# Output projection of a hybrid backbone step: its weight pieces split two ahead through a fourth buffer pair, and the down-projection's fourth pair used only from the third step on

## The chip, the cores and the metric

The kernel runs on one core of one Trainium2 chip. The metric is device microseconds of one execution. The kernel before took 3248.36 us, the median of three runs (3247.75, 3248.36 and 3250.61 us). The profile below is of one more execution, which took 3247.33 us; its span, from the first to the last recorded instruction, is 3245.6 us.

## The reference, cut to what matters

One layer of a backbone works on 640 tokens (512 latent tokens and 128 context tokens) of width 2048. The mixer makes `o_a` (RWKV heads, 1024 columns) and `o_b` (gated MLP, 1024 columns). Then come the output projection, a norm and a gated feed-forward of inner width 5632, all in float32:

```
x = x + g1 * (jnp.concatenate([o_a, o_b], axis=-1) @ lp['w_out'])
h = _rmsnorm(x, lp['norm2_g']) * (1.0 + sc2) + sh2
ff = (jax.nn.silu(h @ lp['w_ffn_gate']) * (h @ lp['w_ffn_up'])) @ lp['w_ffn_down']
return x + g2 * ff, s_fin
```

A last RMSNorm follows. The change touches how the weights of `w_out` (its rows for `o_a`) and of `w_ffn_down` are prepared. What is computed stays the same.

## The kernel before, in words

**Number format.** Every float32 operand of a wide matmul is split into a rounded part `hi` and a rest `lo`. ScalarE copies the raw tile into `hi` (`S.copy`, a CAST in the profile), and VectorE subtracts `hi` from the raw tile to give `lo`. Each product is then three matmuls: `hi` of the weights with both parts of the other operand, and `lo` of the weights with its `hi`. In the profile the three have three lines, one for each.

**Pieces.** A piece of weights is a block of 128 columns and up to 512 rows, so a raw tile of 128 x 512 elements. It is loaded by a DMA from SyncE's queue, split, and used by 12 matmuls (4 blocks of 128 rows, three matmuls each, 320 tokens wide), or by 9 where the piece has only 3 blocks. Raw tiles, `hi` and `lo` have three buffers each in a pool called `st`.

**The output projection.** The rows of `w_out` for `o_b` are multiplied earlier, beside the recurrent scan. The stage called the second half here multiplies the other 1024 rows. It loops over two halves `hf` of 320 tokens, over 16 blocks `m` of output columns, and over two pieces `q` of each block, so it handles 64 pieces. Its core is at lines 1661 to 1683:

```
for hf in range(2):
    s = slice(HALF * hf, HALF * hf + HALF)
    for m in range(KB):
        pool = pbig if m % 2 == 0 else pb2
        ps = pool.tile([P, HALF], F32, tag="big", name="big")
        for q in range(2):
            hi, lo = split(w_out[0, 4 * q * P:(4 * q + 4) * P, m * P:(m + 1) * P], 4)
            for k in range(4):
                kb = 4 * q + k
                TE.matmul(ps, hi[:, k, :], o_hi[kb][:, s], start=(kb == 0), stop=False)
                ...
        ...
        add_out(m, [ps, ps], hf)
        ...
        if hf and m % 2:
            first_half(m // 2)
```

`split` (line 391) allocates, loads, casts (398) and subtracts (399). The three matmuls are lines 1670 to 1672. `add_out` (1292) adds the result to the residual `x1T`. After each block the square of the new residual goes into a sum over all columns (ones matmul, line 1654), and when a token half is complete its reciprocal root `rs` is made (1657 to 1659: VectorE, ScalarE, VectorE). In the second token half `first_half(j)` norms the first one: GpSimd multiplies by `rs` (1605), VectorE scales and shifts (1606), and `operand` splits the result (`xo`: ScalarE 1595, VectorE 1596).

The operand blocks `o_hi[kb]`, `o_lo[kb]` (`oh`, `ol` in the profile) come from the scan. The last two, kb = 6 and 7, come out of its last chain: GpSimd norms `Y` (1486), TensorE transposes it into `pO` (1494), VectorE adds it to `bv` (1498), a gate matmul follows (1512, 1513), `bv` is stored to `d_o` (1516) and loaded back as `ol` (1265, split at 1266 and 1267). The first pieces of the stage lie beside this chain.

**The feed-forward.** Both its products are made by a seven-product scheme (four quarter matrices, 7 products, in the order 1, 2, 3, 7, 5, 6, 4). `seven` (matmuls 1826 to 1828) keeps two split pieces ahead of the one in use by calling `parts` (cast 1635, subtraction 1636); GpSimd makes the differences of weights (`t3`, and `raw`, `rawd` in place, line 1730).

`parts` picks the pool: `pool, kw = (gus[-1], dict(bufs=1)) if gus and next(turn4) == 3 else (st, {})`. So while the list `gus` is not empty, every fourth piece gets a fourth pair of buffers, from the last pool in `gus`.

**From gate/up to down.** When the last gate/up step ends, its helper pool `gu` is closed and the memory is used again: by the pool `dh` with the fourth pair for the down-projection (line 2022, put into `gus` at once) and by `dn` with the accumulators `acc`. `gu` held, among others, the tiles `sp` that the last step splits (1946, 1947) and stores with a DMA to `d_os` (1949). The down-projection then runs 48 steps of seven products; in steps 0 and 1 a product is one piece of 9 matmuls. Each product is copied into `acc` (ScalarE 2044, VectorE 2046 the first time), its operands `xd` are loaded (1865, 1871) and split (1878, 1879), and there are eight banks for products.

**What sets the order.** Within this part the code is written in program order and a scheduler of the framework places the instructions on each engine, using a buffer or a bank as soon as it is free in its own plan. Each engine then executes its list in order, and waits are semaphores.

Of the kernel before, what the change touches and what calls it, by code (L numbers as in the profile page):

```python
# [10 lines left out]
F32 = mybir.dt.float32  # L11
F32R = mybir.dt.float32r
# [7 lines left out]
P = 128  # L20
D = 2048
KB = D // P
# [296 lines left out]
def flow_step(ctx: ExitStack, tc, x_prompt, x_sample, state_rwkv, c, c_ctx, w_mod, b_mod,  # L319
# [3 lines left out]
    nc = tc.nc  # L323
    V, S, G, TE = nc.vector, nc.scalar, nc.gpsimd, nc.tensor
# [22 lines left out]
    for h in range(2):  # L347
        s = slice(CH * h, CH * h + CH)
# [40 lines left out]
    st = ctx.enter_context(tc.tile_pool(name="st", bufs=3, side="right"))  # L389

    def split(src, nk):

        n = 512 // nk
        raw = st.tile([P, nk, n], F32, tag="raw", name="raw", bufs=3)
        hi = st.tile([P, nk, n], F32R, tag="hi", name="hi")
        lo = st.tile([P, nk, n], F32R, tag="lo", name="lo")
        nc.sync.dma_start(raw, src.rearrange("(k p) n -> p k n", p=P))
        S.copy(hi, raw)
        V.tensor_sub(lo, raw, hi.bitcast(F32))
        return hi, lo  # L400
# [884 lines left out]
    def add_out(m, halves, hf=None):  # L1285

        for (lo, hi, v) in ((0, HALF, 0), (HALF, LAT, 0), (LAT, T, 1)):
            if hf is not None and lo // HALF != hf:
                continue
            dst = x1T[m][:, lo:hi]  # L1290
            o = HALF * (lo // HALF)
            V.scalar_tensor_tensor(out=dst, in0=halves[lo // HALF][:, lo - o:hi - o], scalar=modc[2][:, m, v:v + 1],
                                   in1=dst, op0=ALU.mult, op1=ALU.add)

    with ExitStack() as ph:
# [17 lines left out]
        for k in (1, 3):  # L1313
            s = slice(32 * k, 32 * k + 32)
# [300 lines left out]
    PW, READY, gus = [], [], []  # L1615
# [23 lines left out]
    with ExitStack() as ph:  # L1639
        np_ = ph.enter_context(tc.tile_pool(name="np", bufs=2))  # L1640
        pss = ph.enter_context(tc.tile_pool(name="pss", bufs=1, space=PSUM))
        pb2 = ph.enter_context(tc.tile_pool(name="pb2", bufs=2, space=PSUM))
        ones = np_.tile([P, P], F32, name="ones", bufs=1)
        V.memset(ones, 1.0)
        V.tensor_scalar_add(modc[4], modc[4], 1.0)
        V.tensor_tensor(out=modc[4], in0=modc[4],
                        in1=prm[:, C_N2:C_N2 + KB].unsqueeze(2).to_broadcast([P, KB, 2]), op=ALU.mult)
        ss = [pss.tile([P, HALF], F32, name=f"ss{hf}") for hf in range(2)]
        sqs = []

        def stats():

            hf, m, sq = sqs.pop()
            TE.matmul(ss[hf], ones, sq, start=(m == 0), stop=(m == KB - 1))
            if m == KB - 1:
                s = slice(HALF * hf, HALF * hf + HALF)
                V.tensor_scalar(rs[:, s], ss[hf], 1.0 / D, RMS_EPS, op0=ALU.mult, op1=ALU.add)
                S.activation(rs[:, s], rs[:, s], AF.Sqrt)
                V.reciprocal(rs[:, s], rs[:, s])

        for hf in range(2):
            s = slice(HALF * hf, HALF * hf + HALF)
            for m in range(KB):
                pool = pbig if m % 2 == 0 else pb2
                ps = pool.tile([P, HALF], F32, tag="big", name="big")
                for q in range(2):
                    hi, lo = split(w_out[0, 4 * q * P:(4 * q + 4) * P, m * P:(m + 1) * P], 4)
                    for k in range(4):
                        kb = 4 * q + k
                        TE.matmul(ps, hi[:, k, :], o_hi[kb][:, s], start=(kb == 0), stop=False)  # L1670
                        TE.matmul(ps, hi[:, k, :], o_lo[kb][:, s], start=False, stop=False)
                        TE.matmul(ps, lo[:, k, :], o_hi[kb][:, s], start=False, stop=(kb == 7))
                if hf and m == KB - 1:
                    for _ in range(3):
                        next(first)
                if sqs:
                    stats()
                add_out(m, [ps, ps], hf)
                nc.sync.dma_start(d_x1[m][:, s], x1T[m][:, s])
                sq = np_.tile([P, HALF], F32, tag="sq2", name="sq2")  # L1680
                S.activation(sq, x1T[m][:, s], AF.Square)
                sqs.append((hf, m, sq))
                if hf and m % 2:
                    first_half(m // 2)
        for _ in range(2):
            READY.append(parts(PW.pop(0)))
        stats()
# [104 lines left out]
    def fresh(i):  # L1792

        return pP.tile([P, 512], F32, tag="P", name=f"P{i}")[:, 0:HALF], False
# [224 lines left out]

    gus.append(ctx.enter_context(tc.tile_pool(name="dh", bufs=1)))
    dn = ctx.enter_context(tc.tile_pool(name="dn", bufs=1))
    acc = dn.tile([P, 8, 7 * HALF], F32, name="acc")
    sse = dn.tile([P, NT, 8], F32, name="sse")
# [26 lines left out]
    def load_x1(n):  # L2052
        if n >= 0:
            xqs[n] = [xap.tile([P, T], F32, tag=f"x1_{(1, 9)[m]}", name="x1d") for m in range(2)]
            for m in range(2):
                nc.sync.dma_start(xqs[n][m], d_x1[2 * n + m])
# [71 lines left out]

    held = {}
    for s, (c, n) in enumerate(steps):  # L2130
        b11, b21, b22, b12 = ([WD.pop((s, b))] for b in ("11", "21", "22", "12"))
        dloads = itertools.chain(dloads, load_down(s + 2))
        final, turn, after = c == NC - 1, s % 8 == 7 and c < NC - 1, s % 8 == 0 and c > 0
        if final or turn and c == NC - 2:
            bank = lambda i, n=n: filled(n, i)
        elif after:
            bank = lambda i: (held[i], True)
        elif turn:
            def bank(i):
                held[i], _ = fresh(i)  # L2140
                return held[i], False
        else:
            bank = fresh
        if c >= NC - 2 and (final or turn):
            lag[0] = LAST_LAG
        then = [(s + 1, b) for b in ("11", "21")] if s + 1 < len(steps) else ()
        for o in seven(b11, b12, b21, b22, lambda i, k: XD[i, k], None if turn else Last(n) if final else Sum(n),
                       CHK[c], bank, not turn, then):
            if turn:
                if o == 1:  # L2150
                    ops = load_ops(c + 1)
                    next(ops)
                if o in AT:
                    next(ops)
            elif s % 8 == 0 and o in BT:
                next(ops)
            if o > 2:
                next(dloads, None)
            if final and after and o == 2:
                load_x1(n)  # L2160
            while later and o >= later[0][0]:
                later.pop(0)[1]()
            if s == len(steps) - 1 and o == 5:
                while hooks:
                    hooks.pop(0)()
# [52 lines left out]
```

## Time and profile before

| | |
|---|---|
| median of three runs | 3248.36 us |
| profiled execution, own time | 3247.33 us |
| profiled execution, span | 3245.6 us |
| TensorE's mean granted clock | 0.978 |
| end of the scan, start of the stage on `w_out` | 1361.4 us in the span |
| last matmul of the sums in that stage | 1525.9 us |
| first matmul of the down-projection | 2629.3 us |
| last one of it | 3218.9 us |

Times are counted from the start of the span. In a timeline a row gives the start, the duration, the engine, the line and what is done; a bracket behind it gives how long the engine sat idle before it and what ended that wait (for a wait on several things, the last one by the profile). In a table of windows each row is a stretch of the span with the busy time of each engine and the number of its instructions, then TensorE's granted clock as a share, the DMA engines' share and GB/s. PE is TensorE, DVE VectorE, ACT ScalarE, POOL GpSimd, SP SyncE.

### The profile page before, as it was taken

The numbers are of one execution on the slowest core, as the hardware profiler recorded it, in microseconds if no ns is written. First come the engines' busy times: TensorE is split into PE (matmuls) and PEld (weight loads), VectorE is DVE, ScalarE is ACT, GpSimd is POOL, SyncE is SP. The second block draws the span as 40 slices with busy tenths as digits, with TensorE's granted clock in tenths as the row PEclk, the third lists the DMA queues.
The fourth block names the chain that finished last, engine by engine and source line by source line (L and its number), as shares of the span: only waits on it lengthen the run. The fifth ranks groups of instructions, "written<-read, shape, count | busy, mean of one in ns | idle before, by whom it ended". The sixth has DMA issues, their size and how long they took to land. (4 is left out here: it accounts for less than half of the span.)

```text
span 3245.6 us, 73506 instructions
## 1 busy us (share of the span) xinstructions
PE 3108.7 (96%) x28828; PEld 2883.5 (89%) x28828; DVE 2322.3 (72%) x4073; ACT 1444.0 (44%) x3161; POOL 1251.2 (39%) x1082
## 2 busy tenths in 40 slices
PE   6899999999998999999999999999999989999996
PEld 3698888888886877798999999999999989999996
DVE  4456767767756576647977787878878777877787
ACT  3244554555543333335644444444444444444365
POOL 0001222222320032302266566656656644555543
PEclk8899999999998999999999999999999999999998
DMA  8768787887986677455434434433343354553453
GB/s 321 254 182 237 208 227 205 235 233 194 234 226 202 206 219 227 148 150 171 126 107 127 127 108 123 122 117 117 119 124 119 108 175 148 160 165 118 137 169 120
DMA packets 741923, 553.01 MB, mean 170 GB/s; under 512 B 141688, under 2 KB 674184, under 8 KB 732744
## 3 DMA queue, kind: packets, MB, share of 16 engines
q1 hardware_dynamic: 729256, 534.62, 55.5%
q0 software_dynamic: 9984, 13.13, 1.7%
q8 instruction: 227, 3.72, 0.5%
q14 instruction: 120, 0.98, 0.1%
q10 hardware_dynamic: 2336, 0.57, 0.1%
HBM read 438.77 MB, written 111.69 MB: 170 GB/s over the span
## 5 line engine op out<-in xcount | busy, mean ns | idle before, releaser
L1828 PE MATMUL P<-xo,lo 128*128 128x320 f32 x2352 | 727.4, 309 | 3.2 <-DVE lo L1636 3.2
L1827 PE MATMUL P<-xo,hi 128*128 128x320 f32 x2352 | 727.9, 309 | 0.0
L1826 PE MATMUL P<-xo,hi 128*128 128x320 f32 x2352 | 727.7, 309 | 0.0
L1636 DVE TENSOR_TENSOR lo<-raw,hi 128x512 fp32r<-128x512 f32 x532 | 512.9, 971 | 162.6 <-ACT hi L1635 160.5
L1635 ACT CAST hi<-raw 128x512 fp32r<-128x512 f32 x532 | 330.2, 622 | 505.1 <-PE P L1827 430.9
L1828 PEld LDWEIGHTS P<-xo,lo 128*128 128x128 f32 x2352 | 441.9, 188 | 3.9 <-DVE lo L1636 3.7
L1826 PEld LDWEIGHTS P<-xo,hi 128*128 128x128 f32 x2352 | 442.2, 188 | 0.0
L1827 PEld LDWEIGHTS P<-xo,hi 128*128 128x128 f32 x2352 | 442.1, 188 | 0.0
L1730 POOL TENSOR_TENSOR raw<-raw 128x512 f32<-128x512 f32 x252 | 413.5, 1644 | 13.6 <-DVE lo L1636 0.6
L106 PE MATMUL big<-h_hi,hi 128*128 128x320 f32 x1280 | 417.8, 326 | 0.9 <-ACT praw L1209 0.9
L1826 PE MATMUL P<-xd,hi 128*128 128x320 f32 x1232 | 382.6, 311 | 17.3 <-DMA rawd<-in_w_ffn_down_dram 12.1
L106 PE MATMUL big<-h_lo,hi 128*128 128x320 f32 x1280 | 394.1, 308 | 0.0
L106 PE MATMUL big<-h_hi,lo 128*128 128x320 f32 x1280 | 394.0, 308 | 0.0
L1828 PE MATMUL P<-xd,lo 128*128 128x320 f32 x1232 | 382.5, 310 | 3.3 <-DVE lo L1636 3.0
L1827 PE MATMUL P<-xd,hi 128*128 128x320 f32 x1232 | 381.6, 310 | 0.0
L1730 POOL TENSOR_TENSOR t<-raw 128x512 f32<-128x512 f32 x84 | 130.7, 1556 | 452.2 <-DMA raw<-in_w_ffn_up_dram 403.6
L1635 ACT CAST hi<-rawd 128x512 fp32r<-128x512 f32 (+1 forms) x288 | 166.2, 586 | 233.5 <-PE P L1827 165.5
L106 PEld LDWEIGHTS big<-h_hi,hi 128*128 128x128 f32 x1280 | 240.7, 188 | 32.7 <-issue 25.9
L1826 PEld LDWEIGHTS P<-xd,hi 128*128 128x128 f32 x1232 | 232.1, 188 | 20.0 <-ACT hi L1635 14.6
L1636 DVE TENSOR_TENSOR lo<-rawd,hi 128x512 fp32r<-128x512 f32 (+1 forms) x288 | 214.1, 749 | 43.6 <-ACT hi L1635 37.4
L106 PEld LDWEIGHTS big<-h_lo,hi 128*128 128x128 f32 x1280 | 240.7, 188 | 1.2
L106 PEld LDWEIGHTS big<-h_hi,lo 128*128 128x128 f32 x1280 | 240.1, 188 | 0.0
(370 smaller groups left out, 6284.3 us busy)
## 6 DMA issues: line engine op xcount, KB each, us to landing
wt<-in_w_mod_dram SPq DMA_DIRECT2D x96, 1024.0 KB
raw<-in_w_ffn_gate_dram SPq DMA_DIRECT2D x182, 256.0 KB
raw<-in_w_ffn_up_dram SPq DMA_DIRECT2D x182, 256.0 KB
rec<-d_S SPq DMA_DIRECT2D x80, 576.0 KB
raw<-in_w_in_dram SPq DMA_DIRECT2D x172, 256.0 KB
rawd<-in_w_ffn_down_dram SPq DMA_DIRECT2D x128, 256.0 KB
raw<-in_w_out_dram SPq DMA_DIRECT2D x96, 256.0 KB
xd<-d_os SPq DMA_DIRECT2D x66, 320.0 KB
```

The lines of the kernel that those rows point to most:

```text
L106: self.eng, self.run = eng, lambda: fn(*args, **kw)
L1635: S.copy(hi[:, 0:nk], raw[:, 0:nk])
L1636: V.tensor_sub(lo[:, 0:nk], raw[:, 0:nk], hi[:, 0:nk].bitcast(F32))
L1730: G.tensor_tensor(out=o[:, 0:nk], in0=p[:, 0:nk], in1=q[:, 0:nk], op=ALU.subtract)
L1826: TE.matmul(ps, hi[:, k, :], xk[:, 0, :], start=f, stop=False)
L1827: TE.matmul(ps, hi[:, k, :], xk[:, 1, :], start=False, stop=False)
L1828: TE.matmul(ps, lo[:, k, :], xk[:, 0, :], start=False, stop=l)
```

## The change

The stage on `w_out` no longer calls `split` at the place of use. A generator makes the pieces, in the same order, and two are always made ahead. Every fourth piece gets its `hi` and `lo` from the stage's own pool `np_` (memory that the scan used before), the others from `st` as before. The raw tiles keep three buffers. In the down-projection `dh` is put into `gus` only at step 2, so the first two steps split into the three pairs of `st` alone.

```
+        def fetched_w():
+            for n in range(4 * KB):
+                raw = st.tile([P, 4, P], F32, tag="raw", name="raw", bufs=3)
+                m, q = divmod(n % (2 * KB), 2)
+                nc.sync.dma_start(raw, w_out[0, 4 * q * P:(4 * q + 4) * P, m * P:(m + 1) * P].rearrange("(k p) n -> p k n", p=P))
+                pool, kw = (np_, dict(bufs=1)) if n % 4 == 3 else (st, {})
+                hi = pool.tile([P, 4, P], F32R, tag="hi", name="hi", **kw)
+                lo = pool.tile([P, 4, P], F32R, tag="lo", name="lo", **kw)
+                S.copy(hi, raw)
+                V.tensor_sub(lo, raw, hi.bitcast(F32))
+                yield hi, lo
+
+        pieces_w = fetched_w()
+        soon = [next(pieces_w) for _ in range(2)]
...
-                    hi, lo = split(w_out[0, 4 * q * P:(4 * q + 4) * P, m * P:(m + 1) * P], 4)
+                    hi, lo = soon.pop(0)
+                    soon.extend(itertools.islice(pieces_w, 1))
...
-    gus.append(ctx.enter_context(tc.tile_pool(name="dh", bufs=1)))
+    dh = ctx.enter_context(tc.tile_pool(name="dh", bufs=1))
...
     for s, (c, n) in enumerate(steps):
+        if s == 2:
+            gus.append(dh)
```

Each engine keeps its number of instructions. Line numbers behind the change grow by 15, and by 17 in the loop of the down-projection. Three places move.

First, TensorE at the end of the scan. `Y` is what GpSimd has normed, `big_19077` is the first output block before, `big_19089` and `big_19172` are the first and the third one now. Before:

```order
L1671 MATMUL big_19077<-ol_18963,hi_19097 128x320
L1672 MATMUL big_19077<-oh_18962,lo_19098 128x320
L1494 MATMUL pO_18983<-I2_68,Y_18079 64x64
L1494 MATMUL pO_18983<-J2_13863,Y_18079 64x64
L1494 MATMUL pO_18983<-I2_68,Y_18079 64x64
```

Now:

```order
L1686 MATMUL big_19089<-ol_18963,hi_19085 128x320
L1687 MATMUL big_19089<-oh_18962,lo_19086 128x320
L1685 MATMUL big_19172<-oh_18937,hi_19133 128x320
L1686 MATMUL big_19172<-ol_18938,hi_19133 128x320
L1494 MATMUL pO_18983<-I2_68,Y_18079 64x64
L1687 MATMUL big_19172<-oh_18937,lo_19134 128x320
L1685 MATMUL big_19172<-oh_18942,hi_19133 128x320
L1686 MATMUL big_19172<-ol_18943,hi_19133 128x320
```

A whole piece (12 matmuls) of the third block moved in front of and among the first transposes of `Y`; a second one (6 of its matmuls) stands between the first 20 and the second 20 transposes, and 3 more matmuls behind them. In all 21 matmuls moved ahead of the gate matmuls of the last chain.

Second, VectorE in the second token half, around the reciprocal root of the first. `lo_19868` is the second piece of block 2 before; now that piece is `lo_19828`, and `lo_19863` is the first piece of block 3. Before:

```order
L399 TENSOR_TENSOR lo_19850<-raw_19848,hi_19849 128x512
L1659 RECIPROCAL rs2_19061<-rs2_19061 128x320
L1292 SCALAR_TENSOR_TENSOR x1T_13831<-big_19794,modc2_83,x1T_13831 128x192
L1292 SCALAR_TENSOR_TENSOR x1T_13831<-big_19794,modc2_83,x1T_13831 128x128
L1606 TENSOR_SCALAR x1T_13832<-x1T_13832,modc4_85,modc3_84 128x320
L1606 TENSOR_SCALAR x1T_13824<-x1T_13824,modc4_85,modc3_84 128x320
L399 TENSOR_TENSOR lo_19868<-raw_19866,hi_19867 128x512
```

Now:

```order
L1670 TENSOR_TENSOR lo_19828<-raw_19825,hi_19827 128x512
L1659 RECIPROCAL rs2_19061<-rs2_19061 128x320
L1292 SCALAR_TENSOR_TENSOR x1T_13831<-big_19806,modc2_83,x1T_13831 128x192
L1292 SCALAR_TENSOR_TENSOR x1T_13831<-big_19806,modc2_83,x1T_13831 128x128
L1606 TENSOR_SCALAR x1T_13832<-x1T_13832,modc4_85,modc3_84 128x320
L1606 TENSOR_SCALAR x1T_13824<-x1T_13824,modc4_85,modc3_84 128x320
L1670 TENSOR_TENSOR lo_19863<-raw_19860,hi_19862 128x512
```

The other work stands where it stood; each subtraction is one piece further on.

Third, ScalarE where the down-projection begins. `hi_33376` belongs to the second product of step 0, `hi_33381`, `hi_33410` and `hi_33430` to the next three, `hi_33446` to the sixth; `sp` are the last tiles of the gate/up stage. Before:

```order
L1635 CAST hi_33381<-rawd_33319 128x384
L1635 CAST hi_33410<-t3_33369 128x384
L1984 ACTIVATE c_33279<-c_33279 128x640
L1635 CAST hi_33430<-rawd_33321 128x384
L1946 CAST sp_33344<-act_33325 128x320
L1946 CAST sp_33349<-act_33089 128x320
L1878 CAST xd_33400<-opd_33240 128x320
L1878 CAST xd_33403<-opd_33240 128x320
L1878 CAST xd_33406<-opd_33242 128x320
L1946 CAST sp_33354<-act_33325 128x320
L1635 CAST hi_33376<-rawd_33283 128x384
L1635 CAST hi_33446<-rawd_33319 128x384
```

Now:

```order
L1635 CAST hi_33376<-rawd_33283 128x384
L1635 CAST hi_33381<-rawd_33319 128x384
L1999 ACTIVATE c_33279<-c_33279 128x640
L1635 CAST hi_33410<-t3_33369 128x384
L1961 CAST sp_33344<-act_33325 128x320
L1635 CAST hi_33430<-rawd_33321 128x384
L1961 CAST sp_33349<-act_33089 128x320
L1893 CAST xd_33400<-opd_33240 128x320
L1893 CAST xd_33403<-opd_33240 128x320
L1893 CAST xd_33406<-opd_33242 128x320
L1635 CAST hi_33446<-rawd_33319 128x384
L1961 CAST sp_33354<-act_33325 128x320
```

The second product's cast moved from behind the last `sp` cast to the front. Behind these rows six products of the step and three of the next are cast before the first copy into `acc`; and one cast of step 2 (the fourth piece of that step, into `dh`) stands in the middle of step 1, ahead of the cast for step 1's fifth product.

## The prediction

> **What bounds the kernel now.** I read the page's busy table first, then windows over the places where the change moves work, then the timeline around each. The busy table:
>
> ```profile
> PE 3108.7 (96%) x28828; PEld 2883.5 (89%) x28828; DVE 2322.3 (72%) x4073; ACT 1444.0 (44%) x3161; POOL 1251.2 (39%) x1082
> ```
>
> TensorE (PE) is busy 96% of the span. The change takes no matmul away, so it can only win time in which PE stands idle or runs at a lower clock. The windows show where that is (start:end, length, busy us with the count for PE, PEld, DVE, ACT, POOL, then granted clock, DMA share, GB/s):
>
> ```profile
> 1376.00:1397.00 21.00, 15.01 (x133) 13.34 (x134) 5.21 (x9) 2.59 (x4) 4.13 (x5) 0.72 0.19 66
> 1450.00:1460.00 10.00, 10.00 (x67) 9.68 (x66) 4.93 (x9) 5.69 (x9) 0.00 (x0) 1.00 0.58 174
> 1460.00:1470.00 10.00, 7.34 (x36) 6.36 (x35) 9.50 (x10) 3.15 (x6) 8.41 (x9) 0.81 0.16 49
> 1470.00:1480.00 10.00, 9.03 (x50) 8.47 (x48) 10.00 (x16) 4.31 (x9) 8.60 (x8) 0.85 0.45 137
> 1478.00:1526.00 48.00, 47.27 (x300) 44.87 (x300) 32.78 (x72) 23.95 (x47) 0.60 (x1) 1.00 0.56 168
> 2630.00:2640.00 10.00, 0.83 (x6) 0.56 (x4) 7.77 (x14) 5.60 (x13) 4.43 (x4) 0.68 0.78 266
> 2640.00:2650.00 10.00, 7.08 (x35) 6.98 (x36) 3.09 (x6) 2.70 (x6) 3.35 (x3) 0.64 0.92 292
> 2650.00:2670.00 20.00, 20.00 (x138) 20.00 (x138) 15.28 (x25) 9.66 (x21) 9.50 (x8) 1.00 0.33 94
> ```
>
> In the stage on `w_out` PE is full around 1455 (one matmul each 10.00/67 = 0.149 us) and loses 0.73 us in the 48 us from 1478 on. There, splitting earlier has almost nothing to win. Its losses are at the end of the scan (row 1) and in the 20 us from 1460. The down-projection runs at one matmul each 20.00/138 = 0.145 us once started, but nearly all of 2630 to 2640 is lost, and after it the clock is low. Gate/up and down both keep PE full afterwards, so what PE wins at any of these three places is carried to the end.
>
> **The end of the scan.** The timeline of all engines there:
>
> ```profile
> 1375.95 0.47 PE L1494 MATMUL pO<-I,Y 64*64 64x64 f32 x2 [4.63 <-POOL Y L1486]
> 1379.75 0.37 PE L1494 MATMUL pO<-J,Y 64*64 64x64 f32 x1 [3.33 <-POOL Y L1486]
> 1395.06 0.72 ACT L1266 CAST oh<-ol 128x640 fp32r<-128x640 f32 x1
> 1395.21 0.41 PE L1670 MATMUL big<-oh,hi 128*128 128x320 f32 x1 [0.56 <-ACT hi L398]
> 1395.82 0.83 DVE L1267 TENSOR_TENSOR ol<-ol,oh 128x640 fp32r<-128x640 f32 x1
> 1398.24 0.31 PE L1672 MATMUL big<-oh,lo 128*128 128x320 f32 x1
> ```
>
> PE waits 4.63 and 3.33 us for GpSimd's `Y`. Before, 6 pieces (72 matmuls, three blocks without their last operands) are through by 1398.24. After, a seventh piece goes into the waits for `Y`: 12 more matmuls, which are then not owed later, 12 × 0.149 = 1.8 us. Against that, 9 of the 21 moved matmuls stand between the transposes and the gate matmuls, so on the chain that makes the last `oh` and `ol`. At the low clock there (0.26 each, worked out in the next part) they take 9 × 0.26 = 2.3 us. About half of it falls into waits of the chain, so I take 1.1. Net: −0.7 us. Bounds: −2.4 if the chain isn't delayed at all and the 0.56 us wait at 1395.21 goes as well; +2.1 if all 2.3 us count and the fourth pair's first cast makes the last `oh` later by a cast and a subtraction (0.72 + 0.83): 2.3 + 1.55 − 1.8.
>
> **The second token half.** The timeline where the first half's norm begins:
>
> ```profile
> 1459.36 2.15 DVE L1659 RECIPROCAL rs<-rs 128x320 f32<-128x320 f32 x1 [1.33 <-ACT rs L1658]
> 1461.59 17.01 POOL L1605 TENSOR_TENSOR x1T<-x1T,rs 128x320 f32<-128x320 f32 x16 [81.22 <-DVE rs L1659]
> 1464.32 1.34 DVE L399 TENSOR_TENSOR lo<-raw,hi 128x512 fp32r<-128x512 f32 x1
> 1465.71 0.42 PE L1672 MATMUL big<-oh,lo 128*128 128x320 f32 x1 [1.91 <-DVE lo L399]
> 1467.73 2.62 DVE L399 TENSOR_TENSOR lo<-raw,hi 128x512 fp32r<-128x512 f32 x2
> 1469.14 0.63 PE L1672 MATMUL big<-oh,lo 128*128 128x320 f32 x1 [0.75 <-DVE lo L399]
> 1477.92 0.41 PE L1672 MATMUL big<-oh,lo 128*128 128x320 f32 x1 [0.97 <-DVE lo L399]
> ```
>
> GpSimd works 17 us at a stretch on `x1T`, and in that time a subtraction takes 1.34 us on VectorE. VectorE is full from 1470 to 1480, and PE waits for `lo` three times: 1.91 + 0.75 + 0.97 = 3.63 us, which is all that PE is idle in the two windows (20 − 7.34 − 9.03). The low clock adds to it:
>
> ```profile
> 1466.00:1473.00 7.00, 6.25 (x24) 5.85 (x24) 7.00 (x9) 2.19 (x5) 7.00 (x8) 0.51 0.42 123
> ```
>
> 24 matmuls took 6.25 us, 0.26 each instead of 0.149: 24 × 0.11 = 2.7 us. Together 6.3 us are lost. The change adds no work and takes none from VectorE; it puts each `lo` one piece ahead of its use, 12 × 0.149 = 1.8 us of cover, once. The first wait (1.91) shrinks to about 0.1; but VectorE, which is the bound until 1480, still falls behind by the rest, 3.63 − 1.8 = 1.8 us, only later. So of the waits 1.8 goes. For the clock I add only 0.2, because a wait of similar length comes some microseconds later: −2.0 us. Bounds: −6.3 if everything goes, +1.3 if a `lo` moved ahead only pushes back `add_out` and a bank by its 1.34 us. The raw tiles stay at three, so loads are asked for no earlier than a cast and subtraction free them; DMA is at 0.16 to 0.58 here and is no bound.
>
> **Into the down-projection.** All engines where the step begins:
>
> ```profile
> 2630.52 0.31 PE L1828 MATMUL P<-xd,lo 128*128 128x320 f32 x1
> 2630.54 1.29 DVE L1879 TENSOR_TENSOR xd<-opd,xd 128x320 fp32r<-128x320 f32 x3 [1.08 <-ACT xd L1878]
> 2631.13 0.51 ACT L1635 CAST hi<-rawd 128x384 fp32r<-128x384 f32 x1
> 2634.51 0.55 DVE L1636 TENSOR_TENSOR lo<-rawd,hi 128x384 fp32r<-128x384 f32 x1
> 2637.46 1.95 DVE L1879 TENSOR_TENSOR xd<-opd,xd 128x320 fp32r<-128x320 f32 x3
> 2639.43 0.49 SPq L1949 DMA_DIRECT2D d_os<-sp  x1
> 2642.36 0.51 ACT L1635 CAST hi<-rawd 128x384 fp32r<-128x384 f32 x1 [3.60 <-DMA d_os<-sp]
> 2642.40 0.49 DVE L2046 COPY acc<-P 128x320 f32<-128x320 f32 x1 [2.58 <-DMA d_os<-sp]
> 2642.92 0.63 PE L1826 MATMUL P<-xd,hi 128*128 128x320 f32 x1 [12.10 <-DMA rawd<-in_w_ffn_down_dram]
> 2642.90:2650.00 7.10, 7.08 (x35) 6.98 (x36) 2.60 (x5) 2.19 (x5) 2.36 (x2) 0.70 0.95 311
> ```
>
> PE stops at 2630.83 for 12.10 us. Its bracket names a DMA of `rawd`, but PE restarts half a microsecond after ScalarE's cast at 2642.36. That is the second product's, and it had waited for the store of `sp`, because the fourth pair lies in memory that `sp` still held. Three pieces for later products were split meanwhile (the casts from 2631.13 on), and PE, in order, could not use them.
>
> After, the second product's pair comes from `st` and is cast first, where 2631.13 stands. Product 2 then needs its `xd`, ready at 2630.54 + 1.29 = 2631.83, so PE starts at about 2631.9 with 1.1 us lost. Products 3 and 7 have their pairs; the fifth's `lo`, third on VectorE and late behind the `c` and `act` work, ends at about 2638.7 (the row of 2634.51 one place later and behind the casts that free its pair), some 1 us of wait. Product 6 waits for its `xd` until 2637.46 + 1.95 = 2639.41 and ends at about 2641.4, product 4 at 2642.7, and the next step's first takes the eighth bank until 2644.0. The copies into `acc` still wait for the same store (`acc` too lies where `sp` was) until 2642.4, then free a bank each 0.49 us: three by 2643.9, just in time. So by 2650 there have been 113 matmuls: 7 products of 9 by 2642.7 is 54 beyond the first one's 9, and (2650 − 2642.7)/0.145 is 50 more; with the first product's last 9, counted from 2629.3 on, 113. Before, the count is 9 + 35 = 44. The difference of 69 matmuls is 69 × 0.145 = 10.0 us. The several short waits may take 1 us through the clock: −9.0 us. Bounds: all loss before is 12.10 + (7.08 − 35 × 0.145 = 2.0) = 14.1; less the certain 1.1 to 1.3 it is −12.8. At the other end only four pieces (36 × 0.145 = 5.2) get done before everything waits for the same store again, and a first copy (0.49) stands ahead of the next `lo`: −4.7.
>
> [...] The row at 1465.71 shows a wait of 1.91 us, and the window from 1466 has a granted clock of 0.51. A wait of 0.97 us at 1477.92 left it at 1.00 (window 1478:1526). [...]
>
> The change adds a wait too. The fourth piece of step 2 is now the first in the new pair, and its cast stands on ScalarE ahead of the cast for step 1's fifth product. It needs a difference made by GpSimd from a late load:
>
> ```profile
> 2638.89 0.45 SPq L1850 DMA_DIRECT2D rawd<-in_w_ffn_down_dram  x1
> 2641.85 1.00 POOL L1730 TENSOR_TENSOR t<-rawd 128x384 f32<-128x384 f32 x1 [3.59 <-DMA rawd<-in_w_ffn_down_dram]
> 2648.86 7.42 SPq L1850 DMA_DIRECT2D rawd<-in_w_ffn_down_dram  x3
> ```
>
> From issue to GpSimd's use it took 2641.85 − 2638.89 = 2.96 us. If SyncE issues the load when the raw tile is free, about 2642.3, the difference is there at 2642.3 + 2.96 + 1.0 = 2646.3 and the two casts are done at 2647.3. PE, with work until about 2647.9, doesn't notice.
>
> **The sum.** −0.7 − 2.0 − 9.0 = −11.7 us. Against the profiled execution's 3247.33 us (span 3245.6) that is 3235.6; the median of the runs is 1.0 higher, 3248.36, which gives 3236.6 us. Of this kernel's time 0.2%, some 6.5 us, is about what a measurement can tell from no change.
>
> **Rivals.**
> *The stage on `w_out` gives nothing.* It is full at 1455 and nearly so after 1478, and in between VectorE, not the order of splitting, is the limit. For it: VectorE's 10.00 of 10.00. Against it: the largest wait is the first, and there VectorE had work waiting that could have stood earlier. 3248.36 − 9.0 = 3239.4.
> *The stage gives back all that it lost.* If the first wait doesn't happen, the clock stays up and the next two are small: 1.8 + 6.3 + 9.0 = 17.1, so 3231.3. Against it speaks the same full VectorE.
> *The transition's wait is only passed on* to the copies into `acc`, which are released by the same store at 2642.40: −4.7 in place of −9.0, so 3241.0 (3243.7 if the stage gives nothing besides). Against it: there are eight banks, and only seven products before the copies.
> *Slower: ScalarE is blocked by the early cast.* If the load for the new pair is issued only where the late SP row stands, at 2648.86 + 7.42 = 2656.28, the difference is there at 2656.28 + 2.96 + 1.0 = 2660.2, and two casts of 0.51 later PE goes on at 2661.3. It waited from 2647.9, so 13.4 us, and pays the clock's 2.0 again: 15.4 − 11.7 = +3.7, so 3252.1, and 3254.8 or more if the stage gives nothing. It turns to a loss once that difference lands later than about 2656.5 (9.7 us of wait). For it: the DMA engines are at 0.95 in 2642.9:2650. Against it: the raw tiles free earlier when products run earlier, and so loads are issued earlier too.
> That the change does not do what it says is excluded for the transition: ScalarE's list after the change has the second product's cast in front of the `sp` casts.
>
> **How the numbers follow.** Forecast 0.48; stage gives nothing 0.23; stage gives all 0.12; passed on 0.12; blocked 0.05. Faster by over 0.2% means below 3241.9: the first three cases but for 0.03 of their weak ends, and half of the passed-on case: 0.86. Slower by over 0.2% is above 3254.9, the worse part of the blocked case: 0.03. The remaining 0.11 lies between. The range leaves out the blocked case, the weak part of the passed-on one and the strong part of the full recovery: 3229.5 to 3243.5.
>
> **What would show it.** In the trace after, ScalarE should cast the second product's piece near 2631 (less what was won before) without a wait for `d_os`, and PE's wait of 12.10 should be broken into waits of about 1 us; the first copy into `acc` should still wait for that store. In the stage on `w_out` the first wait for `lo` near 1465 should be under 0.5 us, with some 1.8 us of waits left later, and 84 matmuls of its first blocks should be through by the time the last `oh` is cast. I am wrong if PE has a wait of over 3 us at ScalarE's cast or the `acc` copies in step 1, if the waits for `lo` come back with their full 3.6 us, or if the gain in the transition is lost again before 2700.

## The result and the profile after

The changed kernel takes 3240.32 us (median of 7 runs, 3237.72 to 3242.84); the kernel before, beside it, 3248.36 us. The ratio is 0.9978, with a 95% interval of 0.9968 to 0.9988, so between 3.9 and 10.4 us were won. The forecast was 11.7 us: 3236.6 us, with a range of 3229.5 to 3243.5. The profiled execution took 3242.84 us, with a span of 3241.1 us. A few executions of e9 and e11 below were disturbed and took thousands of microseconds more; the ratios leave them out, but e11's profiled execution was one of them.

Two executions also differ in places that the change leaves alone. I therefore cut the span at five events that every kernel has, and compare the stretches between them. For the changed kernel they are these rows: GpSimd's first operation of the last norm of `Y`, the reciprocal root of the first token half, the first gate/up matmul, the first matmul of the down-projection, and the first one of its final block.

```profile
1370.20 0.26 POOL L1474 TENSOR_SCALAR ys<-ys 128x10 f32<-128x10 f32 x1 [11.82 <-PE pG L1512]
1456.97 2.15 DVE L1659 RECIPROCAL rs<-rs 128x320 f32<-128x320 f32 x1 [1.39 <-ACT rs L1658]
1523.60 0.41 PE L1764 MATMUL C<-xo,hi 128*128 128x320 f32 x1 [0.58 <-DVE rs L1657]
2627.45 0.31 PE L1841 MATMUL P<-xd,hi 128*128 128x320 f32 x1
3077.38 0.31 PE L2140 MATMUL P<-xd 128*128 128x320 f32 x1
```

And the three of the kernel before that have not been shown (its reciprocal stands at 1459.36; its first down matmul, which has no bracket, at 2629.35):

```profile
1368.67 0.26 POOL L1474 TENSOR_SCALAR ys<-ys 128x10 f32<-128x10 f32 x1 [11.81 <-PE pG L1512]
1526.96 0.42 PE L1749 MATMUL C<-xo,hi 128*128 128x320 f32 x1 [0.59 <-DVE rs L1657]
3082.84 0.46 PE L2125 MATMUL P<-xd 128*128 128x320 f32 x2
```

| us | norm to reciprocal | to gate/up | gate/up | down, to its final block | the rest of the span |
|---|---|---|---|---|---|
| before | 90.69 | 67.60 | 1102.39 | 453.49 | 162.8 |
| changed | 86.77 | 66.63 | 1103.85 | 449.93 | 163.7 |

The three places gave 3.9 + 1.0 + 3.6 = 8.5 us. The profiled pair differs by only 4.5 us, because this execution came to the first event 1.5 us later and lost 1.5 us in gate/up and 0.9 at the end. All of that lies in stretches whose instructions the change doesn't touch. The 1.5 us in gate/up are a wait for `lo` that both kernels have (2.60 us before, ending at 1592.10; 2.59 in the changed one, ending at 1588.73), with more time at half clock behind it in the changed one (6.83 us in place of 3.41). So the sum of the stretches is nearer to the difference of the medians (8.0 us) than this pair's spans are.

**The end of the scan.** The same window as before's, then PE's waits there and the cast of the last `oh`:

```profile
1376.00:1397.00 21.00, 17.14 (x152) 14.90 (x152) 6.53 (x11) 3.89 (x7) 5.60 (x7) 0.86 0.36 112
```

```profile
1377.49 0.47 PE L1494 MATMUL pO<-I,Y 64*64 64x64 f32 x2 [3.61 <-POOL Y L1486]
1381.30 0.36 PE L1494 MATMUL pO<-J,Y 64*64 64x64 f32 x1 [0.37 <-POOL Y L1486]
1394.27 0.73 ACT L1266 CAST oh<-ol 128x640 fp32r<-128x640 f32 x1 [1.99 <-DMA ol<-d_o]
```

The two waits for `Y` were 4.63 and 3.33 us and are now 3.61 and 0.37: most of the second is filled with matmuls. The granted clock rose from 0.72 to 0.86. The last `oh` is cast 1394.27 − 1370.20 = 24.1 us after GpSimd begins the norm; before it was 1395.06 − 1368.67 = 26.4. So the chain got shorter by 2.3 us, though matmuls were put into it.

**The second token half.** The two windows, and every wait of PE in them:

```profile
1460.00:1470.00 10.00, 8.07 (x50) 7.23 (x49) 9.88 (x12) 3.19 (x8) 10.00 (x11) 1.00 0.30 93
1470.00:1480.00 10.00, 7.08 (x45) 6.21 (x43) 10.00 (x17) 4.64 (x10) 6.55 (x6) 1.00 0.45 136
```

```profile
1463.35 0.42 PE L1687 MATMUL big<-oh,lo 128*128 128x320 f32 x1 [0.53 <-DVE lo L1670]
1466.78 0.42 PE L1687 MATMUL big<-oh,lo 128*128 128x320 f32 x1 [1.40 <-DVE lo L1670]
1475.76 0.81 PE L1654 MATMUL ss<-sq,ones 128*128 128x320 f32 x2 [2.85 <-ACT sq L1696]
```

The waits add up to 4.78 us, more than the 3.63 before. The first is short, as expected; the last is for a square whose `x1T` stands late on the full VectorE. What was won is the clock: 1.00 all through, after a wait of 2.85 us, where before it had fallen to 0.51 after 1.91. Whether the change brought that about is taken up under e3, e4 and e9.

**Into the down-projection.** The windows of before from the first down matmul on, 20.65 us and then 24.35 us, and the same of the changed kernel:

```profile
2629.35:2650.00 20.65, 8.55 (x46) 8.20 (x45) 10.97 (x21) 8.29 (x19) 7.79 (x7) 0.67 0.86 281
2650.00:2674.35 24.35, 24.35 (x168) 24.35 (x168) 18.48 (x30) 11.76 (x26) 13.64 (x12) 1.00 0.29 83
```

```profile
2627.45:2648.10 20.65, 16.57 (x103) 14.76 (x101) 16.93 (x29) 11.45 (x27) 11.29 (x10) 1.00 0.79 255
2648.10:2672.45 24.35, 22.21 (x137) 21.69 (x138) 14.59 (x27) 10.14 (x23) 9.91 (x10) 0.93 0.39 118
```

In the first stretch the change gets 103 − 46 = 57 more matmuls through, 57 × 0.145 = 8.3 us. In the second it loses 168 − 137 = 31 of them again, 4.5 us. The waits, and the rows behind the late ones:

```profile
2629.66 0.41 PE L1841 MATMUL P<-xd,hi 128*128 128x320 f32 x1 [0.72 <-ACT hi L1635]
2634.31 0.41 PE L1843 MATMUL P<-xd,lo 128*128 128x320 f32 x1 [1.09 <-DVE lo L1636]
2636.71 0.42 PE L1843 MATMUL P<-xd,lo 128*128 128x320 f32 x1 [0.82 <-DVE lo L1636]
2639.46 0.42 PE L1843 MATMUL P<-xd,lo 128*128 128x320 f32 x1 [0.85 <-DVE lo L1636]
2648.67 0.42 PE L1843 MATMUL P<-xd,lo 128*128 128x320 f32 x1 [1.02 <-DVE lo L1636]
2660.39 0.41 PE L1841 MATMUL P<-xd,hi 128*128 128x320 f32 x1 [1.18 <-ACT hi L1635]
```

```profile
2645.97 0.51 ACT L1635 CAST hi<-t 128x384 fp32r<-128x384 f32 x1 [2.13 <-POOL t L1745]
2646.39 0.51 ACT L1635 CAST hi<-rawd 128x384 fp32r<-128x384 f32 x1
2647.25 1.36 DVE L1636 TENSOR_TENSOR lo<-rawd,hi 128x384 fp32r<-128x384 f32 x1
2656.72 1.01 POOL L1745 TENSOR_TENSOR t<-rawd 128x384 f32<-128x384 f32 x1 [7.25 <-DMA rawd<-in_w_ffn_down_dram]
2657.81 3.05 POOL L1745 TENSOR_TENSOR rawd<-rawd 128x384 f32<-128x384 f32 x3
2659.82 0.51 ACT L1635 CAST hi<-rawd 128x384 fp32r<-128x384 f32 x1 [5.50 <-POOL rawd L1745]
```

The one wait of 12.10 us is gone, and four of about 1 us stand in the first 12 us. The cast at 2645.97 is the one of step 2 that now goes into the fourth pair: it holds ScalarE for GpSimd, the cast behind it is done at 2646.9, its `lo` takes 1.36 us and ends at 2648.6, and PE waits 1.02 us. The last wait is for the sixth product of step 2: its cast at 2659.82 waited for a difference that GpSimd made in the row of 2657.81, as the second of three. In GpSimd's list the first difference `t` of step 3 (each step has one `t`) stands ahead of it, and GpSimd could begin that one only at 2656.72, when its load had landed. Behind the wait the clock is low:

```profile
2662.00:2665.50 3.50, 3.50 (x16) 3.50 (x15) 2.04 (x6) 1.74 (x5) 0.09 (x1) 0.51 0.57 168
```

### The profile page after: what moved, and what is told of

The parts are those of the page before. It is cut to its first block, busy times and chain, and to the rows that moved or that the text cites. A ratio compares the mean times of both kernels' runs of the same rounds, so it can differ in the third digit from the quotient of the medians.

```text
span 3241.1 us, 73534 instructions
## 1 busy us (share of the span) xinstructions
PE 3112.3 (96%) x28828; PEld 2882.4 (89%) x28828; DVE 2321.6 (72%) x4073; ACT 1442.3 (45%) x3161; POOL 1248.3 (39%) x1082
## 5 line engine op out<-in xcount | busy, mean ns | idle before, releaser
L1843 PEld LDWEIGHTS P<-xd,lo 128*128 128x128 f32 x1232 | 232.0, 188 | 12.2 <-DVE lo L1636 12.1
```

The lines of the kernel that those rows point to most:

```text
L1843: TE.matmul(ps, lo[:, k, :], xk[:, 0, :], start=False, stop=l)
```

## Experiments

Theory T, from the comparison above: the scan's end gives 3.9 us, the second half 1.0, the down-projection 3.6. Its rivals are named with each run. Ratios are to the kernel before, run beside each kernel; the stretches are those of the table above, from each kernel's own trace.

| kernel | ratio (95%) | norm to reciprocal | to gate/up | down |
|---|---|---|---|---|
| changed | 0.9978 (0.9968 to 0.9988) | 86.8 | 66.6 | 449.9 |
| e1 w_out part alone | 0.9984 (0.9976 to 0.9993) | 87.5 | 66.6 | 454.2 |
| e2 down part alone | 0.9984 (0.9976 to 0.9993) | 90.2 | 69.2 | 446.9 |
| e3 e1, two ahead from block 6 | 0.9985 (0.9975 to 0.9995) | 86.5 | 68.0 | 452.6 |
| e4 e1 without the fourth pair | 0.9994 (0.9986 to 1.0003) | 90.5 | 66.2 | 452.2 |
| e5 pair from step 1 | 0.9959 (0.9947 to 0.9972) | 86.5 | 66.6 | 448.5 |
| e6 no pair in down | 0.9999 (0.9990 to 1.0007) | 86.2 | 66.7 | 455.6 |
| e7 pair kept open | 0.9953 (0.9941 to 0.9965) | 86.3 | 68.0 | 448.5 |
| e8 norm on VectorE | 0.9942 (0.9928 to 0.9955) | 86.9 | 60.5 | 449.3 |
| e9 e3 with the pair late too | 1.0009 (0.9997 to 1.0021) | 90.8 | 68.0 | 453.3 |
| e10 e7 and e8 | 0.9945 (0.9929 to 0.9960) | 88.1 | 60.5 | 446.7 |
| e11 changed, again | 0.9973 (0.9961 to 0.9986) | | | |

A stretch whose instructions are the same scatters by one to two us (453.5, 454.2, 452.6, 452.2 and 453.3 in down for the five kernels that have the old transition).

**e1 and e2: each part alone.** e1 leaves the lines on `dh` as before; e2 has only them:

```
-    gus.append(ctx.enter_context(tc.tile_pool(name="dh", bufs=1)))
+    dh = ctx.enter_context(tc.tile_pool(name="dh", bufs=1))
...
     for s, (c, n) in enumerate(steps):
+        if s == 2:
+            gus.append(dh)
```

> Only the part on w_out: the pieces are split two ahead with a fourth pair; the down-projection's fourth pair is used from its first step as before. Theory T (from the two traces): the scan's end gives 3.9 us and the second token half 1.0 us, so 4.9 us below the kernel before, with the wait of about 12 us before the second product of the down-projection still there. Rival P (the prediction's sizes): 2.7 us below. Rival N: the w_out part gives nothing, within 1 us of the kernel before. Between GpSimd's first operation of the last norm and the reciprocal root of the first token half, T expects 86.8 us in place of 90.7, P 90.0, N 90.7.

> Only the part on w_ffn_down: the fourth pair is used from step 2 on, the stage on w_out as before. Theory T: 3.5 us below the kernel before, because the one wait of 12 us becomes some seven waits of 0.4 to 1.2 us for hi and lo, with a stretch at half clock behind them. Rival P: 9 us below, the waits in the trace after being particular to that run. Loss of TensorE from the first down matmul on for 45 us: T 10 us, P 5 us, against 14.3 before.

Each came out at 0.9984, 5.2 us (2.3 to 7.8). For e1 that fits T's 4.9, and P's 2.7 is just inside the interval; the first stretch (87.5, expected 86.8 by T, 90.0 by P) decides for T. For e2 the down stretch is 446.9 us, 6.6 less than before, and 5.3 to 7.3 less than in the five kernels with the old transition. Its first window has the 103 matmuls of the changed kernel, but the second has 152, not 137, at a clock of 1.00:

```profile
2624.32:2644.97 20.65, 16.56 (x103) 14.74 (x101) 16.84 (x28) 11.44 (x27) 11.40 (x10) 1.00 0.81 258
2644.97:2669.32 24.35, 22.86 (x152) 22.34 (x153) 15.12 (x29) 10.80 (x26) 9.60 (x10) 1.00 0.43 130
```

PE's loss in these 45 us (time beyond one matmul each 0.145 us) is 8.0 us, between T's 10 and P's 5. e8 below has the changed kernel's down-projection too. There the waits at step 2 are the same, too, and the clock behind them is 1.00:

```profile
2653.50 0.42 PE L1841 MATMUL P<-xd,hi 128*128 128x320 f32 x1 [1.18 <-ACT hi L1635]
2654.45 0.41 PE L1843 MATMUL P<-xd,lo 128*128 128x320 f32 x1 [0.38 <-DVE lo L1636]
2656.04:2659.45 3.41, 3.41 (x25) 3.41 (x25) 3.01 (x7) 1.46 (x4) 0.87 (x1) 1.00 0.47 140
```

So the low clock after step 2's wait is not bound to the order of instructions; it is that execution's. Without it the down part is worth some 5 to 6.5 us, still not 9: P's size falls.

**e3, e4 and e9: the fourth pair or the splitting ahead.** In e3 and e9 `soon` starts empty and is filled two ahead only from block 6 on; e9 also has the pair only late. e4 has no fourth pair:

```
-                    hi, lo = soon.pop(0)
-                    soon.extend(itertools.islice(pieces_w, 1))
+                    if not soon:
+                        soon.append(next(pieces_w))
+                    hi, lo = soon.pop(0)
+                    if hf or m >= 6:
+                        soon.extend(itertools.islice(pieces_w, 2 - len(soon)))
```

```
-                pool, kw = (np_, dict(bufs=1)) if n % 4 == 3 else (st, {})
+                pool, kw = st, {}                                                       (e4)
+                pool, kw = (np_, dict(bufs=1)) if n % 4 == 3 and n >= 12 else (st, {})  (e9)
```

> The w_out part alone, but the pieces of blocks 0 to 5 of the first token half are made one at a time at their place of use, as before; two ahead and the fourth pair begin at block 6. The end of the scan is then ordered as before. Theory T (the scan's end carries the gain): 1.0 us below the kernel before, 3.9 us above the w_out part alone; the stretch from GpSimd's last norm to the reciprocal root takes 90.7 us as before. Rival H (the gain is from the fourth pair during the second token half): as fast as the w_out part alone, 4.9 us below.

> The w_out part alone without its fourth pair: two pieces are asked for ahead, but only three pairs exist. Theory T (the pair count is what lets a seventh piece pass ahead of the last chain's transposes): within 1.0 us of the kernel before. Rival C (writing the split ahead in the code is what moves it, the pair does not matter): as fast as the w_out part alone, 4.9 us below.

> The w_out part alone, with both the pieces two ahead from block 6 on and the fourth pair from piece 15 on (e3 had that pair from piece 3 on, so it still changed the end of the scan). Theory F (the fourth pair, at the end of the scan, carries the gain, by 24 matmuls in time that was idle): the stretch from GpSimd's last norm to the reciprocal root is back at 90.5 us (before 90.7, changed kernel 86.8), with TensorE's waits of 4.6 and 3.3 us for Y back. Rival H (the pair gains in the stretch's later part): 87 us.

e3's edit, unlike its expectation, left the fourth pair in use from piece 3, and its first stretch was as short as e1's (86.5 us). e4, with everything asked for two ahead but three pairs, was back at 90.5 us and at a ratio that includes 1. e9, with the pair out of the scan's end, had 90.8 us and 1.0009. PE's waits for `Y` in e9 are the old ones:

```profile
1370.57 0.47 PE L1494 MATMUL pO<-I,Y 64*64 64x64 f32 x2 [4.63 <-POOL Y L1486]
1374.38 0.37 PE L1494 MATMUL pO<-J,Y 64*64 64x64 f32 x1 [3.33 <-POOL Y L1486]
```

The gain of the stretch is the fourth pair's, and it is made at the end of the scan. Writing the split ahead changes nothing there by itself: up to the reciprocal root, e4's list for TensorE is that of the kernel before. This fits a scheduler that already split as soon as a pair was free.

For the second half the table shows no gain of the pair. Seven kernels have the changed order there. Four of them (changed, e1, e5, e6) keep the full clock and take 66.6 or 66.7 us; three (e3, e7, e9) have the same waits, drop to half clock once for 3.4 us and take 68.0. Without the pair, e4 keeps the full clock and takes 66.2; before and e2 lose it and take 67.6 and 69.2. So the 1.0 us between before and the changed kernel is within what the clock of an execution makes of it, and a gain by the change is not shown; whether it makes the loss of clock rarer can't be told from so few executions.

**e5, e6 and e7: the pair in the down-projection.** e5 has `if s == 1` in place of `if s == 2`; e6 leaves that line and the next away, so that three pairs are used to the end; e7 opens the pool ahead of gate/up's and keeps it:

```
+    dh = ctx.enter_context(tc.tile_pool(name="dh", bufs=1))
     gu = gux.enter_context(tc.tile_pool(name="gu", bufs=2))
-    gus.append(gu)
+    gus.extend([gu, dh])
...
-    gus.clear()
+    gus.pop(0)
...
-    dh = ctx.enter_context(tc.tile_pool(name="dh", bufs=1))
...
-        if s == 2:
-            gus.append(dh)
```

> The changed kernel, with the fourth pair of the down-projection in use from step 1 instead of step 2. Theory T (what hurt before was one cast that waited for the store of sp with work behind it): in step 1 the pair's first cast comes when that store is nearly done, so the down stretch (first down matmul to the first one of the final block) is within 1 us of the changed kernel's 449.9. Rival Q (any use of that memory in the first two steps stops ScalarE in order): 2 us or more longer than the changed kernel's.

> The changed kernel without the fourth pair in the down-projection at all, three pairs through all 48 steps. Theory T (the pair costs only where its memory isn't free): 450 us for the down stretch as in the changed kernel, since TensorE is full from step 3 on. Rival W (the pair is what keeps TensorE full later): waits for lo through the steps, 3 us or more longer.

> The changed kernel, but the fourth pair of gate/up gets a pool of its own that stays open, so the down-projection uses it from its first step and it waits for no store. Theory T (the remaining waits of 0.7 to 1.2 us are pieces split too late by VectorE and ScalarE, and one more piece of cover hides most of them): TensorE's loss in the first 45 us of the down-projection falls from 10.2 to about 5 us, the down stretch from 449.9 to about 445. Rival D (they come from the order of VectorE's other work and from late loads, which a fourth pair doesn't move): within 1.5 us of the changed kernel's 449.9.

e5: 448.5 us, not slower than with step 2, against Q; it is 1.4 us shorter where T allowed 1. In step 1 the cast that held ScalarE isn't there, and PE's 1.02 us wait is gone with it. Its windows show 108 and 157 matmuls, 25 more than the changed kernel:

```profile
2622.70:2643.35 20.65, 17.05 (x108) 15.51 (x107) 16.45 (x28) 10.98 (x26) 11.44 (x11) 1.00 0.74 237
2643.35:2667.70 24.35, 23.63 (x157) 22.80 (x156) 15.09 (x31) 11.55 (x27) 9.27 (x9) 1.00 0.51 150
```

e6: T was wrong. With three pairs to the end the down stretch is 455.6 us and the kernel is as slow as before. The waits for `lo` are spread over the whole projection (PE's groups; the last part is the idle time before them), first e6, then the changed kernel:

```profile
L1843 PE MATMUL P<-xd,lo 128*128 128x320 f32 x1229 | 383.8, 312 | 20.8 <-DVE lo L1636 20.2
```

```profile
L1843 PE MATMUL P<-xd,lo 128*128 128x320 f32 x1232 | 383.5, 311 | 8.3 <-DVE lo L1636 8.2
```

That is 20.2 − 8.2 = 12 us more of waiting over the projection, and the last two stretches together are 10.1 us longer (455.6 + 168.1 in place of 449.9 + 163.7); rival W holds.

e7: 448.5 us, where T expected 445 and D 449.9 within 1.5 us. That is just inside D's range, and the loss in the first 45 us fell from 10.2 to 7.6 us, where T expected about 5. But e10 below has the same down-projection and took 446.7 us, outside D's range, so one execution of each does not decide. In e7 all of the loss is in the first window, and the second is full, as it was before the change:

```profile
2621.56:2642.21 20.65, 15.91 (x90) 14.37 (x89) 16.57 (x27) 10.78 (x25) 11.22 (x10) 0.92 0.77 241
2642.21:2666.56 24.35, 24.35 (x168) 24.35 (x168) 17.13 (x30) 11.71 (x28) 10.56 (x10) 1.00 0.52 153
```

Four pairs from the start did not remove the first waits in e7. The gain over before is 168 + 90 − 168 − 46 = 44 matmuls, 6.4 us in place of (137 + 103 − 214) × 0.145 = 3.8.

**e8 and e10: what fills VectorE in the second half.** e8 is the changed kernel with one line changed; e10 is e7 and e8 together:

```
-            G.tensor_tensor(out=x[:, t1], in0=x[:, t1], in1=rs[:, t1], op=ALU.mult)
+            V.tensor_tensor(out=x[:, t1], in0=x[:, t1], in1=rs[:, t1], op=ALU.mult)
```

> The changed kernel, with the products of x1T and rs in the first half's norm (16 of 1.06 us on GpSimd) made by VectorE. Theory T (GpSimd at work makes VectorE's two-input operations take twice as long there, 1.34 in place of 0.69 us, and that causes the waits for lo): VectorE gains more than the 16 x 0.49 = 7.8 us it takes over, and the stretch from the reciprocal root to the first gate/up matmul falls from 66.6 to about 63.5 us. Rival V (VectorE is full there anyway, so more work on it makes it later): 70 us or more.

> The changed kernel with both edits that shortened a stretch: the pair kept open (e7) and the norm's products on VectorE (e8). If the two are independent: 60.5 us from the reciprocal root to gate/up, 448.5 us for the down stretch, and some 20 to 22 us below the kernel before. If the better stage only moves the loss on, as fast as e8.

e8 took the 16 products off GpSimd and gave them to VectorE, which was full. The stretch to gate/up fell from 66.6 to 60.5 us, and PE is full for 20 us from the reciprocal root on. The window of the changed kernel, then that of e8:

```profile
1457.00:1477.00 20.00, 15.15 (x92) 13.46 (x91) 19.50 (x23) 7.24 (x15) 17.34 (x16) 1.00 0.32 98
```

```profile
1457.70:1477.70 20.00, 20.00 (x130) 19.20 (x129) 19.15 (x42) 11.12 (x22) 0.00 (x0) 1.00 0.56 169
```

VectorE is as busy, but does 42 instructions in place of 23. Its groups from 1457 to 1475 (mean ns after the comma) for the changed kernel and for e8:

```profile
L1670 DVE TENSOR_TENSOR lo<-raw,hi 128x512 fp32r<-128x512 f32 x5 | 6.2, 1234 | 0.0
L1596 DVE TENSOR_TENSOR xo<-x1T,xo 128x320 fp32r<-128x320 f32 x4 | 4.5, 1160 | 0.0
```

```profile
L1670 DVE TENSOR_TENSOR lo<-raw,hi 128x512 fp32r<-128x512 f32 x9 | 6.2, 686 | 0.8 <-ACT hi L1669 0.6
L1596 DVE TENSOR_TENSOR xo<-x1T,xo 128x320 fp32r<-128x320 f32 x5 | 2.3, 485 | 0.0
```

The operations took 1.23 and 1.16 us beside GpSimd and take 0.69 and 0.49 without it. Rival V falls.

e10 measured 0.9945 (0.9929 to 0.9960): not clear of e8 (0.9942) or e7 (0.9953), and a gain of 18 us (13 to 23) that does not exclude the sum expected (20 to 22). The stretch to gate/up is e8's 60.5 and the down stretch, 446.7, is 1.8 us shorter than e7's, but the first one took 88.1 and gate/up 1104.5 us, more than in e7 or e8. That it is faster than e8 is not shown.

**e11: the changed kernel again.**

> The changed kernel itself once more, for the scatter of the stretches: theory T expects 86.8 +- 0.5 us to the reciprocal root, 66.6 +- 1 us to gate/up, and 447 to 450 us for the down stretch, where the half clock behind the last wait is a matter of chance; the time some 8 us below the kernel before. If the half clock belongs to the program's order, 449.9 again.

0.9973, 8.8 us (4.5 to 12.7), in agreement with the first measurement. It has no trace from which the stretches could be read. What it was to tell about the half clock in step 2 is answered by e2 and e8, which run the changed kernel's down-projection at full clock there.

## Why the prediction was right, and where its sizes were off

The direction was right, the first and the third place gained by the mechanism forecast, and 8.0 us lie inside the range. The sum came nearer than its terms, and that much is luck: the first was 3.2 us too small, the third 5.4 too large, and of the second no gain is shown.

- **The end of the scan, −0.7: measured −3.9 (e9, without the pair: none).** The step that failed is "12 more matmuls, which are then not owed later", with 1.1 us off for the chain. In the trace, 21 us after GpSimd began the norm, 54 matmuls of the stage have been issued in place of 22, and at 40 us 149 in place of 125: two pieces ahead, not one, 24 × 0.149 = 3.6 us. And the 9 matmuls in the chain did not delay it: its last gate matmul stands at 1388.3 − 1370.2 = 18.1 us in place of 1388.6 − 1368.7 = 19.9 (`oh` 2.3 us earlier). They kept PE busy, and the clock was higher (0.86 in place of 0.72). In the eight kernels with the pair at this place the half clock lasts 3.4 or 6.8 us (6.83 in the changed one), in the four without it 10.2 or 13.7 (13.65 before); that the clock is what shortened the chain fits this, but no run holds the order fixed and changes the clock alone. I had priced matmuls put into waits as a delay, and left out that the clock was low over those waits and what came behind them (0.72 in the window from 1376 to 1397).
- **The second half, −2.0: measured −1.0, and not shown to be the change's.** VectorE is the bound, as argued, and what it falls behind shows up later (2.85 us). But the step "of the waits 1.8 goes" failed: they went up from 3.63 to 4.78 us. What the profiled pair won is the clock, for which the sum had only 0.2, and the clock differs between executions of one and the same order (66.6 and 68.0 us). That the stage gives nothing was half of a rival, and for this half the runs bear it out.
- **The transition, −9.0: measured −3.6, or some −5 to −6.5 without that execution's low clock (e2, e5, e8).** The terms for the first 20 us held: 103 matmuls for the predicted 113, 8.3 us for 10.0. The step that failed is that the count at 2650 was taken as the end of the account. Before, the next 24 us were full (168 matmuls); after, they are not (137, and 152 in e2 at full clock). The early cast of step 2 cost 1.02 us at 2648.67: the rival "ScalarE is blocked" at a small price, since I had let the cast end at 2647.3, in time, but not counted the `lo` behind it, which at 1.36 us ends at 2648.6. (The load row shown for that cast, with its difference at 2641.85, is step 1's; as an estimate it held: step 2's `t` was ready at 2645.93 for the 2646.3 forecast.) The 1.18 us in step 2 come from GpSimd's next `t`, step 3's. Counted from the first down matmul it began after 29.3 us (2656.72), and before after 31.8 (2661.15): PE was 8.3 us ahead, this difference only 2.5. In e5, without the early cast, it began after 27.4 us.

```profile
2661.15 1.02 POOL L1730 TENSOR_TENSOR t<-rawd 128x384 f32<-128x384 f32 x1 [4.43 <-DMA rawd<-in_w_ffn_down_dram]
```

- **The rivals.** "Passed on" came nearest in size (−4.7), but not by its mechanism: the copies into `acc` did wait for the store (the first one 0.28 us, until 2641.44), and PE did not wait for them. The clause "wrong if the gain is lost again before 2700" came half true.
- **The clock.** I let a wait of 1.9 us cost clock and took 1 us in all for waits of about 1 us. In the changed kernel 2.85 us cost none, and in step 2 the clock was 0.51 from 2662 on, after waits of 1.18 and 0.40 us. So neither held as a price for a length of wait; the last section shows how the waits lay.

What stays open: why the load for step 3's difference comes only 2.5 us earlier although TensorE begins step 2 about 8 us earlier. e5 points at the early cast for 1.9 us of it; that SyncE's queue stands behind tiles not yet free was argued, not tried.

## What to carry to other kernels

A removed wait is worth what the stages behind it can use: count the work up to where both kernels are full again, not to the end of the wait, since the loads and differences behind it may move forward by less. Where a scheduler already splits as early as buffers allow, code that asks earlier moved next to nothing here; one more buffer pair did (3.9 us of the first stretch), and where it let work into a wait the clock was higher too (0.86 in place of 0.72). When an engine is full, look for who makes its operations long before moving work off it: here VectorE got faster by taking work over from GpSimd (0.69 us for a subtraction in place of 1.23). And before a gain of a microsecond is given to a change, look whether the clock was the same in both executions.

## What the runs showed of the hardware

In these runs the low clock did not go by the length of a wait. Before, 1.91 us of waiting was followed by a granted clock of 0.51; after, 2.85 us by 1.00 and 1.18 plus 0.40 by 0.51; e8 has that last pair of waits (1.18 and 0.38) and kept 1.00. In the profiles before and after, all changes of the granted clock between the first and the last lie on one grid of 3.41 us, so each spell of half clock between them lasted one or more whole steps (3.41 us from 1544.70 before, 6.83 from 1466.19, 13.65 from 1374.03). Here is the 2.85 us wait after the change, cut in two by the grid, and then the step of e7 with most of the same wait, in which PE is idle for 2.04 us:

```profile
1470.83:1474.24 3.41, 2.01 (x12) 1.48 (x11) 3.41 (x4) 0.65 (x2) 3.41 (x4) 1.00 0.26 79
1474.24:1477.65 3.41, 1.89 (x11) 1.73 (x12) 3.41 (x8) 1.86 (x5) 2.31 (x2) 1.00 0.43 131
```

```profile
1468.22:1471.64 3.42, 1.38 (x8) 1.23 (x9) 3.42 (x7) 1.35 (x4) 2.83 (x3) 1.00 0.36 113
1471.64:1475.05 3.41, 3.41 (x15) 3.41 (x14) 3.41 (x9) 1.92 (x6) 0.00 (x0) 0.50 0.62 189
```

PE is busy 59% and 55% of the first two steps, and the clock stays up (1.00); it is busy 40% of e7's step, and the next one runs at half (0.50). From 1360 to 3110 us of the profiles before and after, PE was busy 17 to 54% of each of the 9 steps at full clock that half clock followed, and 55% or more of each of the 997 others. Outside of that stretch the two overlap: in the profile before, a step with 62% (from 1019.05) was followed by half clock and one with 44% (from 70.14) was not. That the same place costs 1.4 us in one execution (68.0) and nothing in another (66.6) fits a wait that falls into one step there and across two here.

Beside GpSimd's products VectorE's subtractions took about twice as long: 1.23 us in place of 0.69 for `lo`, 1.16 in place of 0.49 for `xo`. In e8 the 16 products took 0.48 us each on VectorE (mean of the six up to 1475), where GpSimd, which looked free, had taken 1.12 in the changed kernel, and the stretch was 6.1 us shorter (60.5 us in place of 66.6).
